# Two more plain k tiles ahead of the t2 product, and every output bank added to the residual by VectorE

## The chip, the core and the metric

The kernel runs on one core of a Trainium2 chip. The metric is device microseconds (us) from the start to the end of one execution; the time of the kernel before is the median of three runs, 2190.29 us (2189.22 to 2191.61). Five engines work side by side, each through its own queue in order: TensorE (PE, with its weight loads as PEld), VectorE (DVE), ScalarE (ACT), GpSimd (POOL) and SyncE (SP, which here only issues loads).

## The reference, cut to what matters

Two layers over a residual x of 256 rows by 2048 columns, float32. The change touches only the MLP at the end of each layer:

```python
for l in range(DEPTH):
    ...                                   # attention groups, gating, output projection, residual add
    h = rms_norm(x, mlp_norm_g[l])
    x = x + jnp.square(jax.nn.relu(h @ w_mlp_in[l])) @ w_mlp_out[l]
return rms_norm(x, final_norm_g)
```

Here h @ w_mlp_in is 256x2048 times 2048x8192, and the second product is 256x8192 times 8192x2048.

## The kernel before, in words

**Float32 by halves.** TensorE is fed float32 numbers as two rounded parts, hi and lo. For every pair of k tiles (128 rows of a weight each) of 512 columns, ScalarE copies the raw weights to hi (line 122) and VectorE writes lo = raw - hi (line 123). A product with one k tile is then three matmuls of 512 columns: activations-hi by hi, activations-lo by hi, activations-hi by lo (lines 167 to 169 in `product`, 215 to 217 in `plain`). The third of each three needs lo. The tiles hi and lo have four buffers each, so a new hi waits until TensorE has used the one four pairs earlier.

**Blocks.** The MLP runs in four chunks per layer, each of 2048 hidden columns. A chunk is four calls of `gemm7` (line 173): two that make 1024 hidden columns each, called H0 and H1 here, and two that make 1024 output columns each, called O0 and O1. A call is a block; there are 32, of some 44 us each. Names in the profile that end in h are of H blocks, names that end in o of O blocks.

**Inside a block.** Eight of the sixteen k tiles go through a scheme with seven products instead of eight on 2x2 pieces: the weight pieces b11, b12, b22, b21 (four k tiles each, 1 MB each) and sums of them, made in place by VectorE in b11 (`add`, line 200). The four output banks of PSUM are px, py, pz and pw. The other eight k tiles are plain products, in four calls of `plain(half, i)` per half of the columns, with two k tiles, one hi, one lo and twelve matmuls each. `plain(1, 0)`, `plain(1, 1)`, ... are called p10, p11, p12, p13 here. The start of a block, in the order in which it is written:

- halves of b11 and their product into px; `add(b11, b12)`; ScalarE copies px away (`keep("s1")`)
- halves of b11, now t1, and their product into py; `add(b11, b22)`; `keep("s5")`
- p10 into py and pw; halves of b11, now t2, and their product into px; `keep("v2")`
- p11, p12; the product with b22; p13; the product with t3 (b12 + b22); and so on

In H blocks b12 + b22 is made by a DMA that adds (line 229); in O blocks by VectorE (line 237), written after the product with b22, though it may run as soon as b12 and b22 are in place and b12 has been read.

**What sets the order.** Each engine takes its instructions in an order that a planner fixed when the kernel was built: by estimated times it gives each engine the earliest written instruction that is ready at that moment. So the order in the trace is not that of the text: matmuls of p10 stand among those of t1, for example. Matmuls into one bank keep their written order. `pump` lines between matmuls call pending work (the squared ReLU of the hidden columns and their turn by TensorE, lines 257 to 283).

**The output of an O block.** For each half of the columns (second half first) and each half t of the rows, the bank is scaled by r2 and added to the residual xt (lines 703 to 714): by one VectorE instruction (line 710), except for row half 1 of the first column half, which is bank px, in chunks 0 to 2: there ScalarE writes the scaled bank to a tile y (line 707) and an adding DMA that GpSimd issues adds y to xt (line 708). In the last chunk VectorE does all four. px is the last bank that a block finishes, and the following block starts at once.

Of the kernel before, what the change touches and what calls it, by code (L numbers as in the profile page):

```python
# [28 lines left out]
FCH = 4  # L29
# [12 lines left out]
def trunk(ctx: ExitStack, tc: tile.TileContext, x_in, xT, w_in, w_out, w_mlp_in, w_mlp_out,  # L42
# [22 lines left out]
    def t2(name):  # L65
        return tmp.tile([P, GW], F32, tag="t2", name=name, bufs=4)
# [95 lines left out]
    def product(ps, lhs, parts, start=False):  # L162

        for j, (hi, lo) in enumerate(parts):
            ah, al = lhs(j)
            first, last = start and j == 0, j == len(parts) - 1
            T.matmul(ps, lhsT=ah, rhs=hi, start=first, stop=False, skip_group_check=True)  # L167
            T.matmul(ps, lhsT=al, rhs=hi, start=False, stop=False, skip_group_check=True)  # L168
            T.matmul(ps, lhsT=ah, rhs=lo, start=False, stop=last, skip_group_check=True)  # L169
            if j % 2:  # L170
                pump()

    def gemm7(w, c0, lhs, sums, rest, keep, name, moved=False):

        def rawb(two, half):
            t = stage["mlp"].tile([P, SP, GW], F32, tag="rawb", name=f"rb{two}{half}_{name}", bufs=3)
            src = w[:2 * SP * P, c0 + half * GW:c0 + (half + 1) * GW].rearrange("(k two p) c -> two p k c", two=2, p=P)
            nc.sync.dma_start(t, src[two])
            return t

        def direct(k, t):
            def get(j):
                a, h = lhs[2 * j + k]
                return a[:, h, t * P:(t + 1) * P], a[:, h, S + t * P:S + (t + 1) * P]  # L190
            return get

        def summed(i):
            def get(j):
                e = sums[j]
                return e[:, 0, i], e[:, 1, i]
            return get

        def add(dst, src):
            V.tensor_tensor(dst, dst, src, op=ALU.add)  # L200

        px, py, pz, pw = (psg.tile([P, GW], F32, tag="g", name=f"p{c}_{name}") for c in "xyzw")
        raw = {}

        def plain(half, i):

            if i % 2 == 0:
                raw[half] = load(w, rest[2 * i:2 * i + 4], c0 + half * GW, f"{name}{half}{i}")
            ks = rest[2 * i:2 * i + 2]
            for k, (hi, lo) in zip(ks, halves(raw[half][:, i % 2 * 2:i % 2 * 2 + 2, :], 2, f"{name}{half}{i}")):  # L210
                a, h = lhs[k]
                for t, ps in enumerate(((pz, px), (py, pw))[half]):
                    ah, al = a[:, h, t * P:(t + 1) * P], a[:, h, S + t * P:S + (t + 1) * P]
                    first, last = k == rest[0] and t == half, k == ks[-1]
                    T.matmul(ps, lhsT=ah, rhs=hi, start=first, stop=False, skip_group_check=True)  # L215
                    T.matmul(ps, lhsT=al, rhs=hi, start=False, stop=False, skip_group_check=True)  # L216
                    T.matmul(ps, lhsT=ah, rhs=lo, start=False, stop=last, skip_group_check=True)  # L217
                pump()

        b11, b12 = rawb(0, 0), rawb(0, 1)  # L220
        product(px, direct(0, 0), halves(b11, SP, f"b11{name}"), start=True)
        add(b11, b12)
        keep("s1", px)
        b22 = rawb(1, 1)
        product(py, direct(0, 1), halves(b11, SP, f"t1{name}"), start=True)
        add(b11, b22)
        keep("s5", py)
        if moved:
            G.dma_start(b12, b22, accum_op=ALU.add)
        plain(1, 0)  # L230
        product(px, summed(0), halves(b11, SP, f"t2{name}"))
        keep("v2", px)
        plain(1, 1)
        plain(1, 2)
        product(py, summed(1), halves(b22, SP, f"b22{name}"))
        if not moved:
            add(b12, b22)
        plain(1, 3)
        product(px, summed(2), halves(b12, SP, f"t3{name}"))
        b21 = rawb(1, 0)  # L240
        keep("v3", px)
        plain(0, 0)
        add(b11, b21)
        plain(0, 1)
        product(px, direct(1, 1), halves(b11, SP, f"t4{name}"))
        plain(0, 2)
        product(pz, direct(1, 0), halves(b21, SP, f"b21{name}"))
        plain(0, 3)
        return [[pz, py], [px, pw]]
# [90 lines left out]
    for l in range(DEPTH):  # L340
# [319 lines left out]
        for c in range(FCH):  # L660
            hid, hs = [None] * KT, [None] * SP
            for g in range(2):
                kept = {}

                def keep(what, ps, kept=kept, n=f"{l}{c}{g}"):
                    k = mlp.tile([P, GW], F32, tag="kept", name=f"k{what}h{n}", bufs=4)
                    if what == "v3":
                        V.tensor_tensor(k, kept["s5"], ps, op=ALU.subtract)
                    else:
                        A.activation(k, ps, AF.Copy)  # L670
                    kept[what] = k

                ps = gemm7(w1, c * fw + 2 * g * GW, Want(xm), Want(xs), allk[2 * SP:], keep, f"h{l}{c}{g}", moved=True)
                z11, z12, z22 = kept["s1"], kept["v2"], kept["v3"]
                V.scalar_tensor_tensor(z12, z12, -1.0, ps[0][1], op0=ALU.mult, op1=ALU.add)
                V.tensor_tensor(z22, z22, ps[1][1], op=ALU.add)
                pending.append(hidden(hid, hs, ((z12, z12), (z22, z22)), 8 * g + 4, f"hid{l}{c}{g}b"))
                V.tensor_tensor(z11, z11, ps[0][0], op=ALU.add)
                pending.append(hidden(hid, hs, ((z11, z11), (ps[1][0], None)), 8 * g, f"hid{l}{c}{g}a"))
                if r2 is None:  # L680
                    rm = rstd(ss_m, f"m{l}")
                    r2 = small.tile([P, 4], F32, tag="r2", name=f"r2_{l}", bufs=2)
                    V.tensor_tensor(r2[:, :2], rm, rm, op=ALU.mult)
                    V.tensor_scalar(r2[:, 2:], r2[:, :2], -1.0, None, op0=ALU.mult)
            for g in range(2):
                def xg(t, half, g=g):
                    return xt[t][:, (2 * g + half) * GW:(2 * g + half + 1) * GW]

                kept = {}

                def keep(what, ps, kept=kept, n=f"{l}{c}{g}"):
                    k = mlp.tile([P, GW], F32, tag="kept", name=f"k{what}o{n}", bufs=4)
                    if what == "v3":
                        k = kept["s5"]
                        V.tensor_tensor(k, k, ps, op=ALU.subtract)
                        A.activation(k, k, AF.Copy, scale=r2[:, 1:2])
                    else:
                        i = {"s1": 0, "v2": 2, "s5": None}[what]
                        A.activation(k, ps, AF.Copy, **({} if i is None else {"scale": r2[:, i:i + 1]}))
                    kept[what] = k  # L700

                ps = gemm7(w2[c * fw:(c + 1) * fw], 2 * g * GW, Want(hid), Want(hs), late, keep, f"o{l}{c}{g}")
                for half in (1, 0):
                    for t in range(2):
                        if (t, half) == (1, 0) and c < FCH - 1:
                            y = t2(f"y{l}{c}{g}")
                            A.activation(y, ps[t][half], AF.Copy, scale=r2[:, t:t + 1])
                            G.dma_start(xg(t, half), y, accum_op=ALU.add)
                        else:
                            V.scalar_tensor_tensor(xg(t, half), ps[t][half], r2[:, t:t + 1], xg(t, half),  # L710
                                                   op0=ALU.mult, op1=ALU.add)
                        k = kept.get({(0, 0): "s1", (0, 1): "v2", (1, 1): "v3"}.get((t, half)))
                        if k is not None and c < FCH - 1:
                            G.dma_start(xg(t, half), k, accum_op=ALU.add)
                        elif k is not None:
                            V.tensor_tensor(xg(t, half), xg(t, half), k, op=ALU.add)
                        if c == FCH - 1:
                            square_sum(ss_a, t, 2 * g + half, f"n{l}")
                    if c == FCH - 1 and not fin:
                        q = 2 * g + half  # L720
                        pending.append(turn(xa, xt, q * GW, 4 * q, f"xa{l + 1}_{q}_", C_ATT + (l + 1) * KT))
# [75 lines left out]
```

## Time and profile before

| | before |
|---|---|
| median of three runs | 2190.29 us |
| the profiled execution, its own time | 2193.12 us |
| its span from the first to the last instruction | 2191.4 us |
| PE busy, matmuls | 2133.2 us, 97%, 9500 |
| PEld busy | 1706.9 us, 78% |
| DVE busy | 1712.0 us, 78% |
| ACT busy | 1362.8 us, 62% |
| POOL busy | 73.0 us, 3% |
| mean granted TensorE clock | 0.996 |

Busy times are shares of the span. A matmul's row lasts longer than the distance to the next one, since matmuls overlap; so a loss of TensorE is read from the starts of following matmuls. Idle time in brackets at the end of a row is the time just before it in which the engine had nothing running, with what ended it.

### The profile page before, as it was taken

What the parts mean: (1) busy time and instruction counts of PE and PEld (TensorE: products, weight loads), DVE (VectorE), ACT (ScalarE), POOL (GpSimd) and SP (SyncE); (2) the same over time, 40 slices, a digit from 0 to 9 for tenths busy, and PEclk for the clock granted to TensorE, in tenths of its full rate; (3) what the DMA queues carried; (4) which work ended last, traced back from release to release, by engine and by line L of the source; (5) the groups of instructions that cost most, each with busy time, mean ns of one, the idle gap of its engine ahead of it and who ended that gap; (6) DMA issues with size and microseconds to landing.
All of it is one profiled execution on the core that took longest, in us unless ns stands there. A gap on an engine that the chain in (4) does not pass through costs nothing. (4 is left out here: it accounts for less than half of the span.)

```text
span 2191.4 us, 25750 instructions
## 1 busy us (share of the span) xinstructions
PE 2133.2 (97%) x9500; PEld 1706.9 (78%) x9500; DVE 1712.0 (78%) x2024; ACT 1362.8 (62%) x1903; POOL 73.0 (3%) x90
## 2 busy tenths in 40 slices
PE   9999999999999999999999999999999999999996
PEld 7877888777777777777788778887777777777775
DVE  6665566898898898889965655678988988988897
ACT  6465565675675576667654656556656755755764
POOL 0000000000000000000000000000000000000000
PEclk9999999999999999999999999999999999999999
DMA  8644565567857866766465454656677578568652
GB/s 317 203 144 156 168 229 169 180 212 228 236 167 212 258 207 187 213 217 203 155 215 183 143 157 155 241 147 218 212 225 202 193 231 248 173 192 253 209 191 96
DMA packets 212621, 435.35 MB, mean 199 GB/s; under 512 B 7824, under 2 KB 8464, under 8 KB 210320
## 3 DMA queue, kind: packets, MB, share of 16 engines
q1 hardware_dynamic: 202416, 402.22, 55.9%
q0 software_dynamic: 9216, 29.36, 7.0%
q10 hardware_dynamic: 864, 2.14, 0.3%
q8 instruction: 74, 1.21, 0.2%
q14 instruction: 51, 0.42, 0.1%
HBM read 402.23 MB, written 2.10 MB: 185 GB/s over the span
## 5 line engine op out<-in xcount | busy, mean ns | idle before, releaser
L123 DVE TENSOR_TENSOR lo_wi<-raw_wi,hi_wi 128x1024 fp32r<-128x1024 f32 x160 | 195.1, 1223 | 162.2 <-ACT hi_wi L122 154.6
L122 ACT ACTIVATE hi_wi<-raw_wi 128x1024 fp32r<-128x1024 f32 x160 | 168.9, 1059 | 166.7 <-PE pg_wi L157 156.1
L156 PE MATMUL pg_wi<-hi_wi,xa 128*128 128x512 f32 x640 | 260.4, 407 | 0.0
L158 PE MATMUL pg_wi<-lo_wi,xa 128*128 128x512 f32 x640 | 251.6, 393 | 0.0
L157 PE MATMUL pg_wi<-hi_wi,xa 128*128 128x512 f32 x640 | 251.3, 393 | 0.0
L122 ACT ACTIVATE hi_o<-raw_o 128x1024 fp32r<-128x1024 f32 x128 | 134.8, 1058 | 64.9 <-PE pw_o L216 43.1
L123 DVE TENSOR_TENSOR lo_o<-raw_o,hi_o 128x1024 fp32r<-128x1024 f32 x128 | 153.9, 1222 | 17.7 <-ACT hi_o L122 16.7
L122 ACT ACTIVATE hi_h<-raw_h 128x1024 fp32r<-128x1024 f32 x128 | 134.2, 1054 | 46.9 <-PE pw_h L216 24.4
L123 DVE TENSOR_TENSOR lo_h<-raw_h,hi_h 128x1024 fp32r<-128x1024 f32 x128 | 154.8, 1220 | 7.2 <-ACT hi_h L122 7.2
L200 DVE TENSOR_TENSOR rb_o<-rb_o,rb_o 128x2048 f32<-128x2048 f32 x64 | 146.4, 2288 | 9.6 <-DMA rb_o<-w_mlp_out 9.0
L156 PEld LDWEIGHTS pg_wi<-hi_wi,xa 128*128 128x128 f32 x640 | 120.3, 188 | 29.1 <-issue 7.3
L158 PEld LDWEIGHTS pg_wi<-lo_wi,xa 128*128 128x128 f32 x640 | 120.4, 188 | 25.2
L157 PEld LDWEIGHTS pg_wi<-hi_wi,xa 128*128 128x128 f32 x640 | 120.5, 188 | 22.3 <-issue 0.7
L123 DVE TENSOR_TENSOR lo_wo<-raw_wo,hi_wo 128x1024 fp32r<-128x1024 f32 x64 | 78.4, 1225 | 60.8 <-ACT hi_wo L122 60.8
L200 DVE TENSOR_TENSOR rb_h<-rb_h,rb_h 128x2048 f32<-128x2048 f32 x48 | 109.8, 2288 | 1.3 <-DMA rb_h<-w_mlp_in 0.8
L122 ACT ACTIVATE hi_wo<-raw_wo 128x1024 fp32r<-128x1024 f32 x64 | 67.9, 1060 | 64.0 <-PE pg_wo L157 57.8
L156 PE MATMUL pg_wo<-hi_wo,mix 128*128 128x512 f32 x192 | 76.3, 397 | 0.0
L158 PE MATMUL pg_wo<-lo_wo,mix 128*128 128x512 f32 x192 | 75.1, 391 | 0.0
L157 PE MATMUL pg_wo<-hi_wo,mix 128*128 128x512 f32 x192 | 74.8, 389 | 0.0
L123 DVE TENSOR_TENSOR lo_b11h<-rb_h,hi_b11h 128x1024 fp32r<-128x1024 f32 x32 | 39.2, 1226 | 27.8 <-ACT hi_b11h L122 25.9
L123 DVE TENSOR_TENSOR lo_t1h<-rb_h,hi_t1h 128x1024 fp32r<-128x1024 f32 x32 | 38.7, 1224 | 23.8 <-ACT hi_t1h L122 23.8
L123 DVE TENSOR_TENSOR lo_t3o<-rb_o,hi_t3o 128x1024 fp32r<-128x1024 f32 x32 | 39.0, 1224 | 23.4 <-ACT hi_t3o L122 23.3
(1939 smaller groups left out, 5880.9 us busy)
## 6 DMA issues: line engine op xcount, KB each, us to landing
raw_wi<-w_in SPq DMA_DIRECT2D x80, 1024.0 KB, 5.2
rb_h<-w_mlp_in SPq DMA_DIRECT2D x64, 1024.0 KB, 6.2
raw_h<-w_mlp_in SPq DMA_DIRECT2D x64, 1024.0 KB, 5.6
raw_o<-w_mlp_out SPq DMA_DIRECT2D x64, 1024.0 KB, 6.6
rb_o<-w_mlp_out SPq DMA_DIRECT2D x64, 1024.0 KB, 6.5
raw_wo<-w_out SPq DMA_DIRECT2D x24, 1024.0 KB, 5.1
rb_h<-rb_h POOLq DMA_DIRECT2D x16, 1024.0 KB, 6.9
raw_wo<-w_out SPq DMA_DIRECT2D x16, 512.0 KB, 5.0
```

The lines of the kernel that those rows point to most:

```text
L122: A.activation(hi, raw[:, i:i + m, :], AF.Copy)
L123: V.tensor_tensor(lo, raw[:, i:i + m, :], hi.bitcast(F32), op=ALU.subtract)
L156: T.matmul(ps[t], lhsT=ah, rhs=hi, start=first, stop=False)
L157: T.matmul(ps[t], lhsT=al, rhs=hi, start=False, stop=False)
L158: T.matmul(ps[t], lhsT=ah, rhs=lo, start=False, stop=last)
L200: V.tensor_tensor(dst, dst, src, op=ALU.add)
```

## The change

`plain(1, 1)`, p11, is written ahead of the product with t2 and no longer behind it, in all 32 blocks. The banks px of the O blocks in chunks 0 to 2 (twelve of them) are added to the residual by VectorE in place of ScalarE and the adding DMA.

```diff
         plain(1, 0)
+        plain(1, 1)
         product(px, summed(0), halves(b11, SP, f"t2{name}"))
         keep("v2", px)
-        plain(1, 1)
         plain(1, 2)
...
                     for t in range(2):
-                        if (t, half) == (1, 0) and c < FCH - 1:
-                            y = t2(f"y{l}{c}{g}")
-                            A.activation(y, ps[t][half], AF.Copy, scale=r2[:, t:t + 1])
-                            G.dma_start(xg(t, half), y, accum_op=ALU.add)
-                        else:
-                            V.scalar_tensor_tensor(xg(t, half), ps[t][half], r2[:, t:t + 1], xg(t, half),
-                                                   op0=ALU.mult, op1=ALU.add)
+                        V.scalar_tensor_tensor(xg(t, half), ps[t][half], r2[:, t:t + 1], xg(t, half),
+                                               op0=ALU.mult, op1=ALU.add)
```

## Rows read from the trace of the kernel before

**Rows 1.** The page, busy us, share of the span and instructions of two engines.

```profile
PE   2133.2 (97%) x9500; PEld 1706.9 (78%) x9500; DVE 1712.0 (78%) x2024; ACT 1362.8 (62%) x1903; POOL 73.0 (3%) x90
```

**Rows 2.** Waits of PE: line and releaser, us in total, times, longest.

```profile
PE px_o L167 <- ACT hi_t2o L122: 16.8, 16, 1.6
PE px_h L169 <- DVE lo_t2h L123: 7.4, 14, 0.5
PE pw_o L215 <- ACT hi_o L122: 3.0, 7, 0.4
```

**Rows 3.** Timeline of PE in an O1: start, length, line, output and inputs.

```profile
873.01 0.50 PE L215 MATMUL pw_o<-hi_o,hid021b 128*128 128x512 f32 x1 [0.45 <-ACT hi_o L122]
...
878.55 0.39 PE L217 MATMUL pw_o<-lo_o,hid021b 128*128 128x512 f32 x1
879.44 0.50 PE L167 MATMUL px_o<-hi_t2o,e_hid020a 128*128 128x512 f32 x1 [0.50 <-ACT hi_t2o L122]
879.77 0.40 PE L168 MATMUL px_o<-hi_t2o,e_hid020a 128*128 128x512 f32 x1
880.70 0.50 PE L169 MATMUL px_o<-lo_t2o,e_hid020a 128*128 128x512 f32 x1 [0.53 <-DVE lo_t2o L123]
```

**Rows 4.** Timeline of DVE in the same O1.

```profile
869.68 0.74 DVE L710 SCALAR_TENSOR_TENSOR xt<-pz_o,r,xt 128x512 f32<-128x512 f32 x1
870.35 2.28 DVE L200 TENSOR_TENSOR rb_o<-rb_o,rb_o 128x2048 f32<-128x2048 f32 x1
872.54 2.35 DVE L123 TENSOR_TENSOR lo_t1o<-rb_o,hi_t1o 128x1024 fp32r<-128x1024 f32 x2
...
875.95 2.28 DVE L200 TENSOR_TENSOR rb_o<-rb_o,rb_o 128x2048 f32<-128x2048 f32 x1
879.42 2.36 DVE L123 TENSOR_TENSOR lo_t2o<-rb_o,hi_t2o 128x1024 fp32r<-128x1024 f32 x2 [1.18 <-ACT hi_t2o L122]
```

**Rows 5.** Timeline of ACT in the same O1.

```profile
869.43 0.69 ACT L707 ACTIVATE y<-px_o,r 128x512 f32<-128x512 f32 x1 [3.25 <-PE px_o L217]
870.01 2.00 ACT L122 ACTIVATE hi_t1o<-rb_o 128x1024 fp32r<-128x1024 f32 x2
...
876.42 0.60 ACT L699 ACTIVATE ks5o<-py_o 128x512 f32<-128x512 f32 x1 [2.89 <-PE py_o L169]
878.33 2.01 ACT L122 ACTIVATE hi_t2o<-rb_o 128x1024 fp32r<-128x1024 f32 x2 [1.31 <-DVE rb_o L200]
```

**Rows 6.** Lines 707 and 710: duration in ns (least, median, most), first and last start.

```profile
L707 ACT ACTIVATE y<-px_o,r x12: 690/691/691, 511.7 to 1998.9; 128x512 f32<-128x512 f32 x12
L710 DVE SCALAR_TENSOR_TENSOR xt<-px_o,r,xt x4: 740/746/751, 1048.1 to 2177.1; 128x512 f32<-128x512 f32 x4
```

**Rows 7.** Timeline of PE at t2 in an H0, an H1 and an O0.

```profile
742.62 0.50 PE L167 MATMUL px_h<-hi_t2h,e_xm 128*128 128x512 f32 x1 [0.26 <-ACT hi_t2h L122]
743.88 0.50 PE L169 MATMUL px_h<-lo_t2h,e_xm 128*128 128x512 f32 x1 [0.52 <-DVE lo_t2h L123]
...
789.16 0.50 PE L169 MATMUL px_h<-lo_t2h,e_xm 128*128 128x512 f32 x1 [0.53 <-DVE lo_t2h L123]
...
832.81 0.56 PE L167 MATMUL px_o<-hi_t2o,e_hid020a 128*128 128x512 f32 x1 [1.63 <-ACT hi_t2o L122]
```

**Rows 8.** Timeline of DVE in that H0 and that O0.

```profile
735.72 2.36 DVE L123 TENSOR_TENSOR lo_t1h<-rb_h,hi_t1h 128x1024 fp32r<-128x1024 f32 x2 [0.67 <-ACT hi_t1h L122]
742.60 2.36 DVE L123 TENSOR_TENSOR lo_t2h<-rb_h,hi_t2h 128x1024 fp32r<-128x1024 f32 x2 [1.19 <-ACT hi_t2h L122]
...
828.97 2.28 DVE L200 TENSOR_TENSOR rb_o<-rb_o,rb_o 128x2048 f32<-128x2048 f32 x1
831.17 1.22 DVE L123 TENSOR_TENSOR lo_o<-raw_o,hi_o 128x1024 fp32r<-128x1024 f32 x1
```

**Rows 9.** Busy us in windows, PE PEld DVE ACT POOL, clock, DMA: O0's start, and behind its wait.

```profile
814.00:837.00 23.00, 21.11 (x92) 16.84 (x91) 22.83 (x21) 17.04 (x24) 0.00 (x0) 0.93 0.41 134
...
833.00:836.50 3.50, 3.50 (x9) 2.78 (x9) 3.50 (x4) 1.75 (x3) 0.00 (x0) 0.52 0.02 5
```

## The prediction

> **What bounds the kernel now.** I read the page first, then the waits of TensorE, then the timelines around those waits. The page has TensorE busy for 97% of the span [rows 1], and the kernel has almost nothing else to wait for, so only the places where TensorE stands still can be won back. The waits of PE put nearly all of them at one spot: the first matmuls of the product with t2, which wait for ScalarE's hi (16.8 us) or VectorE's lo (7.4 us in H blocks) [rows 2]. The reader is to see in both rows the same few waits repeated, 16 and 14 times.
>
> The timelines show why. t2 is made in place: VectorE adds b22 to b11 in 2.28 us, which it can only do after lo of t1; then ScalarE makes hi, then VectorE lo. In the O1 shown the add starts at 875.95, hi at 878.33 and lo at 879.42, and VectorE sits idle for 1.18 us before that lo [rows 4, 5]. TensorE has run out of t1 and p10 by 878.55 [rows 3].
>
> A wait costs more than its printed idle time. Following matmuls start 0.23 us apart. From 878.55 to 879.44 are 0.89 us, so 0.66 are lost where 0.50 are printed; from 879.77 to 880.70 are 0.93, so 0.70 for 0.53 [rows 3]. I add 0.17 to every printed idle time below.
>
> **The swap, by kind of block.** p11 adds and removes no instruction. It puts 12 matmuls, 12 x 0.23 = 2.76 us, between p10 and t2, and one hi and one lo ahead of t2's. Two things must hold for it to pay: p11's own halves must be there in time, and what they push back must not be late in turn.
> - Halves: p11's raw weights come with the load of p10. Its hi can go into idle time of ScalarE (2.89 us before 876.42 [rows 5]). Its lo, half of the 2.36 us that two take, comes behind the add, because the add is written earlier; there it falls into the 1.18 us (O1) or 1.19 us (H0) in which VectorE waits for hi of t2 anyway [rows 4, 8]. So lo of t2 is hardly later than now, and the cover is as long as the lo that it hides: were that idle time gone, lo of t2 would be 1.2 us later, which the 2.76 us of p11 still cover.
> - p11's lo is ready some 1.2 us after the add's end, when TensorE has just finished p10. Four of p11's matmuls (two per bank) need hi alone, 0.92 us, so I leave 0.1 to 0.15 us of each wait standing.
>
> H0: waits of 0.26 and 0.52 [rows 7], with two times 0.17 they make 1.12; gain 1.0 each. The 14 waits on lo in H blocks [rows 2] are those of all eight H1 and of six H0 (the H0 of each layer's first chunk shows none): 6.0 us. H1: 0.53 + 0.17 = 0.70, and some tenths among the turns beside it [rows 7]; gain 0.75, eight blocks: 6.0 us. O1 of chunks 0 to 2: 0.66 + 0.70 = 1.36 [rows 3]; gain 1.2, six blocks: 7.2 us. The two O1 of the last chunks have other work between and wait less regularly; bounds 0 and 1.36, I take 0.4: 0.8 us.
>
> O0 is different, and I expect little there. Its wait is the largest, 1.63 + 0.17 = 1.8 us, in eight blocks [rows 7]. But VectorE is busy for 22.83 of the 23 us around it [rows 9], and there the add (828.97) comes ahead of lo of p10 (831.17) [rows 8]. Matmuls of p11 go into the same two banks as p10's and stand behind those that need this lo, which ends only at 832.4, 0.4 us before the wait ends now. So p11 can't fill that wait; bounds are 0 and 1.8, nearest to the rows is 0.4 at most, and I take 0.2: 8 x 0.2 = 1.6 us.
>
> What is late next? The product with b22 and those behind it have their hi bound by free buffers, which TensorE frees, and p12 stays where it was, so nothing behind t2 gets less cover but `keep("v2")`: px is next written by the t3 product, with p12, b22 and p13 between, 36 matmuls or 8.3 us, for a copy like the 0.60 us of `keep("s5")` at 876.42 [rows 5]. I count nothing.
>
> **The second edit.** It removes 12 ScalarE writes of 0.69 us and 12 adding DMAs that nobody waits for, and adds 12 VectorE instructions of 0.75 us [rows 6]. Before the next of its kind starts, one takes 0.67 us (869.68 to 870.35 [rows 4]). Where do they fall? At the start of the next block, behind the one for pz.
> - In the six H0 that follow, VectorE then idles for 0.67 us (735.72 [rows 8]), since ScalarE's y delays hi of t1. The new instruction fills just that: nothing either way.
> - In the six O1, ScalarE's y (869.43) delays hi of t1 and of p10 [rows 5], for which TensorE waits 0.45 + 0.17 = 0.62 us at 873.01 [rows 3]; in total the waits' row has 3.0 us [rows 2]. That wait may go. Against it, VectorE has no idle time there: the add of b12 and b22 (870.35) and lo of t1 (872.54) [rows 4] come 0.67 us later if they keep their order; if the planner finds hi of t1 ready and puts the add behind it, lo of t1 comes 872.54 - 870.35 - 0.67 = 1.5 us earlier. So a block lies between 0.67 lost and 0.62 gained. The wait is a row and the delay only a possibility, so I stay near the row, at 0.5: 3.0 us.
>
> The Trainium skill speaks against this edit: "VectorE: DVE Perf Modes", Specifications, has "VectorE sits closer to SBUF; ScalarE sits closer to PSUM", so that ScalarE would be the engine to empty a bank. The trace agrees, with 0.75 against 0.69 us [rows 6]; by that alone the edit would lose 12 x 0.06 = 0.7 us, if it lay on the path.
>
> **Sum.** 6.0 + 6.0 + 7.2 + 0.8 + 1.6 + 3.0 = 24.6 us. From the profiled execution's 2193.1 us this leaves 2168.5. The median of the runs is 2190.3, 2.8 lower, so I forecast 2165.7.
>
> **The rivals.**
> 1. The O0 wait goes too. If the planner puts lo of p10 ahead of the add there, as the other blocks have it (for O1 the gap from 874.9 to 875.95 [rows 4] is that lo), TensorE has p10 and p11 to do while t2 is made: 8 x 1.6 more instead of 0.2, 11.2 us, and the clock drop that can follow this wait (3.5 us at a granted clock of 0.52, the lower of the two levels, where it is else 1.00 [rows 9]; 1.7 us each time) goes as well. Time 2165.7 - 11.2 = 2154.5 or somewhat less. For it: order is the planner's to choose, and it has p11 to weigh now. Against: neither edit touches what stands ahead of that add in an O0, which follows an H1.
> 2. The wait only changes its name, from t2's halves to p11's lo. If p11's matmuls of hi are not spread over both banks, or its hi is planned late, TensorE waits some 0.7 us at line 217 in the 20 blocks counted for the swap: 14 us less gain, 2179.7. For it: p11's lo stands behind the same add. Against: ScalarE's idle time and the four matmuls without lo.
> 3. Slower: VectorE bounds the start of the blocks. If every microsecond of VectorE there goes through to TensorE, the swap gains nothing, as it changes VectorE's order and not its work, and the second edit costs 12 x 0.67 = 8.0 us: 2198.3. It decides from the point where VectorE has no idle time between lo of t1 and lo of t2. For it: 22.83 of 23 us in O0 [rows 9]. Against: the idle 1.18 and 1.19 us [rows 4, 8], in the blocks where I count most of the gain.
> 4. The change doesn't do what it says: the planner's estimates let t2's matmuls stand ahead of p11's anyway, as it does in O0 with p10's (832.81 is followed by matmuls of p10). Then the time stays, 2190.3.
>
> **How the numbers follow.** Forecast 0.52, rival 1 0.15, rival 2 0.17, rival 3 0.10, rival 4 0.06. The forecast's own range goes up by the second edit at its bound in O1 (6 x 1.17 = 7.0 us) and by nothing gained in O0 and the last two O1 (2.4), to 2175; and down by O0 at 0.4 (1.6), the last two O1 at 1.36 (1.9), the second edit at 0.62 (0.7) and nothing left of the waits at p11 (20 x 0.12 = 2.4), to 2159. To hold 8 in 10 I leave out rivals 3 and 4 and a little at the lower end: 2151 to 2187. A change under 0.2%, 4.4 us, can't be told from none in this kernel's measurement. Faster: 0.52 + 0.15 + 0.17 = 0.84; same 0.06; slower 0.10.
>
> **What would show it.** The waits of PE for hi and lo of t2 in H0, H1 and O1 gone from the list of waits, with at most 0.2 us each on p11's lo; VectorE's idle time before lo of t2 filled by a lo of p11; the O0 wait still there at line 167 or 217, eight times, of 1.2 to 1.8 us. For the second edit: bank px added by VectorE right behind pz, and in O1 the lo of t1 directly behind both, ahead of the add of b12 and b22. The prediction is wrong if new waits of PE at p11 add up to more than 5 us, if the O0 waits vanish, or if the b12 + b22 add turns up between lo of p11 and lo of t2, so that t2 waits again.

## The result, and the profile after

| | before | after |
|---|---|---|
| median of four runs | 2189.76 us (2188.17 to 2191.61) | 2157.11 us (2156.86 to 2160.34) |
| the profiled execution | 2193.12 us | 2156.94 us |

The ratio is 0.9854, with a 95% interval of 0.9837 to 0.9871: 32.7 us faster, where 24.6 were forecast.

The page of the kernel after, busy us, share and instructions; the answer to [rows 1]:

```profile
PE 2115.4 (98%) x9500; PEld 1707.6 (79%) x9500; DVE 1717.3 (80%) x2036; ACT 1354.7 (63%) x1891; POOL 65.3 (3%) x78
```

TensorE does the same 9500 matmuls. VectorE has 12 instructions more and ScalarE and GpSimd 12 fewer each.

The waits of PE in the kernel after (line and releaser, us in total, times, longest); the answer to [rows 2]:

```profile
PE px_o L167 <- ACT hi_t2o L122: 10.1, 9, 1.3
PE px_o L215 <- DVE ks5o L695: 5.9, 15, 0.6
PE py_o L215 <- ACT ks5o L699: 3.0, 9, 1.2
PE pz_o L217 <- DVE lo_o L123: 0.8, 1, 0.8
PE pw_o L215 <- ACT hi_o L122: 0.3, 1, 0.3
```

The wait on lo of t2 in H blocks (7.4 us) is gone. That on hi of t2 is left nine times, and eight of these are the O0 blocks. Of the seven waits for hi of p10 one is left. The second row is the price: before, this wait came 7 times for 2.6 us in all, now 15 times. It is the first plain product into px behind t3, which must wait until VectorE has subtracted the t3 product into `kept` (line 695); I call it the v3 wait.

**Where the time went, by block.** I take each block from its first matmul with b11 to that of the next block, in the two profiled executions. The H0 blocks are shorter by 9.5 us in all (1.3 to 1.4 each in the regular ones), the eight H1 by 8.2 (1.02 each), the six O1 of chunks 0 to 2 by 16.9 (2.8 each), and the very last O1 with its tail by 2.6. The O0 are longer: by 0.5 to 0.7 in six of them, which makes 3.4. The other two are shorter by 1.1 each, because before they held a drop of the granted clock ([rows 9] is one, at 0.52; the other, from 1918.0 to 1921.5, stands at 0.58). In all O0 lose 1.2 us. These, with 0.2 ahead of the first block, make 36.2 us, the difference of the two spans. The execution profiled before was 3.4 us above its median; its two drops make 3.0 of them (those O0 took 47.1 us, the other six 45.6).

Now the same places as in the rows of before. VectorE at the start of an O1 of the kernel after (start, length, line, operation, output and inputs), the answer to [rows 4]:

```profile
856.87 0.74 DVE L705 SCALAR_TENSOR_TENSOR xt<-pz_o,r,xt 128x512 f32<-128x512 f32 x1
857.53 0.74 DVE L705 SCALAR_TENSOR_TENSOR xt<-px_o,r,xt 128x512 f32<-128x512 f32 x1
858.19 2.35 DVE L123 TENSOR_TENSOR lo_t1o<-rb_o,hi_t1o 128x1024 fp32r<-128x1024 f32 x2
860.46 1.22 DVE L123 TENSOR_TENSOR lo_o<-raw_o,hi_o 128x1024 fp32r<-128x1024 f32 x1
861.59 2.28 DVE L200 TENSOR_TENSOR rb_o<-rb_o,rb_o 128x2048 f32<-128x2048 f32 x1
863.79 1.22 DVE L123 TENSOR_TENSOR lo_o<-raw_o,hi_o 128x1024 fp32r<-128x1024 f32 x1
864.93 2.28 DVE L200 TENSOR_TENSOR rb_o<-rb_o,rb_o 128x2048 f32<-128x2048 f32 x1
867.13 2.35 DVE L123 TENSOR_TENSOR lo_t2o<-rb_o,hi_t2o 128x1024 fp32r<-128x1024 f32 x2
```

The reader is to see three things. px is added right behind pz. lo of t1 comes directly behind both, where before the 2.28 us add of b12 and b22 stood between (870.35 in [rows 4]). And that add now stands at 864.93, between lo of p11 and lo of t2. Idle time there is none.

TensorE in the same O1, the answer to [rows 3]:

```profile
867.25 0.40 PE L217 MATMUL pw_o<-lo_o,hid021b 128*128 128x512 f32 x1
867.49 0.39 PE L167 MATMUL px_o<-hi_t2o,e_hid020a 128*128 128x512 f32 x1
867.72 0.39 PE L168 MATMUL px_o<-hi_t2o,e_hid020a 128*128 128x512 f32 x1
867.95 0.40 PE L215 MATMUL py_o<-hi_o,hid021a 128*128 128x512 f32 x1
...
868.65 0.40 PE L169 MATMUL px_o<-lo_t2o,e_hid020a 128*128 128x512 f32 x1
```

The last matmul of p11 and the first of t2 are 0.24 us apart: no wait, where 0.66 and 0.70 us were lost before. The first lo of t2, at 868.65, stands behind three matmuls of p12 (867.95 is the first).

TensorE's waits in the O0 ahead of it, the answer to the last of [rows 7]:

```profile
818.93 0.50 PE L215 MATMUL py_o<-hi_o,hid021b 128*128 128x512 f32 x1 [0.23 <-ACT ks5o L699]
820.91 0.50 PE L167 MATMUL px_o<-hi_t2o,e_hid020a 128*128 128x512 f32 x1 [1.24 <-ACT hi_t2o L122]
841.77 0.50 PE L215 MATMUL px_o<-hi_o,hid021b 128*128 128x512 f32 x1 [0.34 <-DVE ks5o L695]
```

The 1.63 us wait has become 1.24, and two short ones have come beside it. Read by starts against the regular 0.23 us, and with the 0.1 us by which the matmul behind a wait is late too, the loss at t2 fell from 1.8 to 1.5, that at py rose from 0.16 to 0.50, and the v3 wait adds 0.61 that was not there.

### The profile page after: what moved, and what is told of

It is laid out like the page before. It is cut to its first block, busy times and chain, and to the rows that moved or that the text cites. A ratio compares the mean times of both kernels' runs of the same rounds, so it can differ in the third digit from the quotient of the medians.

```text
span 2155.2 us, 25746 instructions
## 1 busy us (share of the span) xinstructions
PE 2115.4 (98%) x9500; PEld 1707.6 (79%) x9500; DVE 1717.3 (80%) x2036; ACT 1354.7 (63%) x1891; POOL 65.3 (3%) x78
## 5 line engine op out<-in xcount | busy, mean ns | idle before, releaser
L122 ACT ACTIVATE hi_b11h<-rb_h 128x1024 fp32r<-128x1024 f32 x32 | 34.0, 1063 | 33.9 <-PE px_h L216 13.3
```

The source lines that it names most:

```text
L122: A.activation(hi, raw[:, i:i + m, :], AF.Copy)
```

## The experiments

Each is a change to the kernel after, unless it says that it undoes a part. The differences of time are those of medians. The kernel before, measured again beside them, took 2191.04 us beside the swap alone, the second edit alone, the edit of p10 and the DMA in all O blocks; 2191.97 beside the kernel without px additions, the swap with a DMA, the copy by ScalarE and the three together; and 2191.32 beside the two fillers. That is up to 2.2 us from the 2189.76 above, so a difference of 1 to 2.4 us from the kernel after rests on the lengths of the blocks in the traces, and the medians only agree with them.

### The swap alone

The output of px goes back to ScalarE and the adding DMA; p11 stays ahead of t2.

> p11 ahead of t2; bank px in chunks 0 to 2 still goes through ScalarE and the adding DMA. Theory A (the two edits add up, each with what the changed kernel shows of it): the swap alone gives H0 6 x 1.3, H1 8 x 1.0, O1 6 x 1.3 and O0 about nothing, 23 us less than before, 2166; in O1 the wait of 0.45 us at 873 stays, and the 0.50 and 0.53 us at t2 go. Theory B (the swap does nearly all, the second edit's VectorE instruction is only hidden): 30 us or more less than before, 2160 or below.

2168.23 us (2167.5 to 2169.12), ratio 0.99 (0.9885 to 0.9915): 22.8 us less than before. H0 gives 8.9, H1 8.1, the six O1 6.8 (1.1 each) and the very last one 2.4; O0 loses 0.7 in sum, which is 0.5 in each of the six undisturbed ones, less what the two drops of before gave back. In O1 the t2 waits are gone and those at t1 stay. VectorE and the wait at the same place:

```profile
685.61 0.74 DVE L710 SCALAR_TENSOR_TENSOR xt<-pz_o,r,xt 128x512 f32<-128x512 f32 x1
686.27 2.28 DVE L200 TENSOR_TENSOR rb_o<-rb_o,rb_o 128x2048 f32<-128x2048 f32 x1
688.47 2.35 DVE L123 TENSOR_TENSOR lo_t1o<-rb_o,hi_t1o 128x1024 fp32r<-128x1024 f32 x2
```

```profile
688.93 0.50 PE L215 MATMUL pw_o<-hi_o,hid011b 128*128 128x512 f32 x1 [0.45 <-ACT hi_o L122]
```

This is the order and the wait of before, to a hundredth [rows 3, 4]. The time is near the 23 us of Theory A. It is also near the 21.6 us that the prediction's terms for the swap make, but that is partly luck: H0, H1 and the last O1 gave 6.7 us more than forecast, and the eight O0, at 0.5 lost each, 5.5 less. The rest of the 32.7 us isn't the swap's.

### The second edit alone

p11 goes back behind t2; VectorE adds px.

> Bank px added by VectorE in all chunks; p11 stays behind t2. Theory A (additive): 9 us less than before, 2181, all of it in the six O1 blocks (1.5 us each). Theory C (the edits need each other: on VectorE the add of b12 and b22 is now planned between the add of b11 and b22 and lo of t2, 2.28 us where 1.18 were idle, and only p11 covers that): the O1 blocks win some 0.9 us at t1 and lose 1.1 us at t2, so 2188 to 2191, with a wait of PE for lo of t2 in O1 of 1.2 to 1.8 us. Forecast of the prediction for this edit: 3 us less.

2187.05 us (2184.93 to 2188.86), ratio 0.9981 (0.9972 to 0.999): 4.0 us less than before. That is close to the 3.0 forecast by luck, since larger gains and losses cancel in it, and between the two theories, nearer to C. But 22.8 and 4.0 make 26.8: the two together bring 5.9 us more than one by one. The blocks say the same: the six O1 give 16.9 us with both edits, 6.8 and 3.8 with one of them. VectorE in an O1 of this kernel (x2 is two of the adds in a row), and TensorE's waits in it:

```profile
694.01 4.48 DVE L200 TENSOR_TENSOR rb_o<-rb_o,rb_o 128x2048 f32<-128x2048 f32 x2
698.41 2.35 DVE L123 TENSOR_TENSOR lo_t2o<-rb_o,hi_t2o 128x1024 fp32r<-128x1024 f32 x2
```

```profile
697.50 0.50 PE L167 MATMUL px_o<-hi_t2o,e_hid010a 128*128 128x512 f32 x1 [0.23 <-ACT hi_t2o L122]
699.39 0.50 PE L215 MATMUL py_o<-hi_o,hid011b 128*128 128x512 f32 x1 [1.16 <-ACT hi_o L122]
```

Here too the add of b12 and b22 has left its place ahead of lo of t1, and the t1 waits (1.3 us per O1) are gone. But it now stands right ahead of lo of t2, and TensorE loses 1.9 us around t2 where it lost 1.6 before, and 0.3 more than before at v3. The long wait printed is on hi of p11 and not on lo of t2, as Theory C had it; but lo of t2 was there only 0.2 us later (698.41 and half of 2.35 us, an estimate). With p11 ahead of t2 the 12 matmuls cover this; that is the interaction.

### Is it VectorE's work or its order: px not added at all

```diff
-                        V.scalar_tensor_tensor(xg(t, half), ps[t][half], r2[:, t:t + 1], xg(t, half),
-                                               op0=ALU.mult, op1=ALU.add)
+                        if (t, half) != (1, 0) or c == FCH - 1:
+                            V.scalar_tensor_tensor(...)
```

> The changed kernel with the twelve additions of bank px in chunks 0 to 2 left out, so that part of the output is missing; neither ScalarE nor VectorE has that work. Theory work (the new VectorE instruction costs up to the 0.67 us that it takes): 0 to 8 us less than the changed kernel, 2149 to 2157. Theory order (the instruction's place is worth more than its time: with it, hi of t1 is ready when VectorE comes free and lo of t1 goes ahead of the 2.28 us add of b12 and b22; without it the planner puts that add first again): slower than the changed kernel, by some 1 us in each of six O1 blocks, 2161 to 2164.

2168.34 us (2166.76 to 2168.97), ratio 0.9894 (0.9879 to 0.9909). With less work it is 11.2 us slower than after. Theory order had the direction right and the size too small (2161 to 2164): an O1 takes 1.7 us more than after, not some 1. VectorE and ScalarE in an O1:

```profile
686.19 0.75 DVE L706 SCALAR_TENSOR_TENSOR xt<-pz_o,r,xt 128x512 f32<-128x512 f32 x1
686.85 2.28 DVE L200 TENSOR_TENSOR rb_o<-rb_o,rb_o 128x2048 f32<-128x2048 f32 x1
689.05 2.35 DVE L123 TENSOR_TENSOR lo_t1o<-rb_o,hi_t1o 128x1024 fp32r<-128x1024 f32 x2
```

```profile
686.39 2.01 ACT L122 ACTIVATE hi_t1o<-rb_o 128x1024 fp32r<-128x1024 f32 x2 [3.70 <-DVE rb_o L200]
```

The add is back ahead of lo of t1, although ScalarE has no y to make. ScalarE starts hi of t1 at 686.39; one of its two instructions takes 1.05 us, so the first half stands at about 687.4 (an estimate from rows). VectorE comes free of pz at 686.85, before that, and the planner gives it the add. With 0.67 us of px behind pz it comes free after it, and lo of t1 is what it gets. These are times of the trace; the planner's own estimates are not on record.

### A filler in the place of the px addition

The 12 instructions stay, with the same shape and length, but read bank pz and write a tile that nobody reads.

```diff
-                        V.scalar_tensor_tensor(xg(t, half), ps[t][half], r2[:, t:t + 1], xg(t, half),
+                        d, u = xg(t, half), t
+                        if (t, half) == (1, 0) and c < FCH - 1:
+                            d, u = t2(f"y{l}{c}{g}"), 0
+                        V.scalar_tensor_tensor(d, ps[u][half], r2[:, u:u + 1], xg(t, half),
```

> The changed kernel without the addition of bank px in chunks 0 to 2 (so part of the output is missing), and in its stead a VectorE instruction of the same form that reads bank pz again and writes a tile that nobody reads. On VectorE it stands where the addition stood, behind that of pz and ahead of lo of t1; the add of b12 and b22 comes later, as in the changed kernel. Theory order (all that the second edit wins is that hi of t1 gets ready in its time): as fast as the changed kernel, 2155 to 2159, although nothing is done. Theory bank (it is bank px being emptied by VectorE that helps): as slow as with the addition left out, 2166 to 2170.

2158.58 us (2157.64 to 2163.32), ratio 0.9857 (0.984 to 0.9875): as fast as after, 9.8 us faster than without any instruction there. Its O1:

```profile
684.52 0.74 DVE L708 SCALAR_TENSOR_TENSOR xt<-pz_o,r,xt 128x512 f32<-128x512 f32 x1
685.19 0.74 DVE L708 SCALAR_TENSOR_TENSOR y<-pz_o,r,xt 128x512 f32<-128x512 f32 x1
685.85 2.35 DVE L123 TENSOR_TENSOR lo_t1o<-rb_o,hi_t1o 128x1024 fp32r<-128x1024 f32 x2
```

A useless instruction brings what the px addition brings. ScalarE's writes of y and the adding DMAs are gone from this kernel and from the one without px additions alike. So what is worth some 10 us is neither the bank, nor ScalarE's relief, nor the DMAs, but 0.67 us of VectorE at this spot, which changes what follows.

### The same filler, reading the slice of xt that pz was just added to

The edit is that of the filler above, with `xg(u, half)` at the end of the line.

> The same as the filler in place, but it also reads what the addition of pz has just written, so the planner puts it between the two lo of t1, with the add of b12 and b22 ahead of both. Theory order: not faster than with the addition left out, 2168, and slower by up to 6 x 0.67 = 4 us: 2166 to 2173. Theory work (what counts is VectorE's work and not its order): the same as the filler in place.

2186.82 us (2185.27 to 2189.19), ratio 0.998 (0.997 to 0.9989). The expectation was missed by far, and for a reason of its own. VectorE in an H0:

```profile
743.57 0.75 DVE L708 SCALAR_TENSOR_TENSOR y<-pz_o,r,xt 128x512 f32<-128x512 f32 x1 [1.59 <-DMA xt<-ks1o]
744.24 1.22 DVE L123 TENSOR_TENSOR lo_h<-raw_h,hi_h 128x1024 fp32r<-128x1024 f32 x1
745.37 2.35 DVE L123 TENSOR_TENSOR lo_t2h<-rb_h,hi_t2h 128x1024 fp32r<-128x1024 f32 x2
```

The slice that the filler reads also gets an adding DMA (`ks1o`). The filler waited for that, and the queue of VectorE behind it: lo of p11 came late, and TensorE waited for it in six H0, 11.0 us in all. So the total decides nothing. In O1 the filler fell between the two lo of t1, behind the add of b12 and b22, and waited for the DMA some 0.2 us in most of them; there only 0.2 us per block was gained over before, where the swap alone gives 1.1. In these blocks the same work costs 0.9 us at one place (0.2 of it the wait for the DMA) and gains at the other, as the order theory has it.

### The swap, with O1's b12 + b22 by a DMA

The px output stays with ScalarE, as in the swap alone; the O1 calls get `moved=g == 1`, so that the disputed add leaves VectorE.

> The swap alone, with bank px still through ScalarE and y, and b12 + b22 made by an adding DMA in O1 only, so that on VectorE lo of t1 follows the add of bank pz directly. Theory order: the O1 blocks win what the second edit won there beside the swap, 1.4 to 1.7 us each, 8 to 10 us less than the swap alone, 2158 to 2160, although ScalarE still makes y first. Theory ScalarE (y, which delays hi of t1 and of p10, is what holds O1's start): the wait of PE for hi of p10 at line 215 stays, and 4 us at most are won, 2164 or more.

2161.47 us (2161.04 to 2163.04), ratio 0.9863 (0.9847 to 0.988): 6.8 us less than the swap alone, and 1.5 more than Theory order allowed. O1 gains 2.2 each in place of 1.1. VectorE in it:

```profile
684.67 0.74 DVE L710 SCALAR_TENSOR_TENSOR xt<-pz_o,r,xt 128x512 f32<-128x512 f32 x1
686.08 2.36 DVE L123 TENSOR_TENSOR lo_t1o<-rb_o,hi_t1o 128x1024 fp32r<-128x1024 f32 x2 [0.67 <-ACT hi_t1o L122]
```

ScalarE's y still delays hi of t1, and VectorE idles for 0.67 us; yet the t1 waits of TensorE are gone. So what made them in O1 was the add ahead of lo of t1, and not the y that the prediction blamed. By starts, the v3 wait of O1 stays at 0.9 us or more here, as in the swap alone; in the kernel after it is 0.45. That part of the second edit's gain does not come with the add's move alone, and what makes it is not shown.

### O0: lo of p10 ahead of the add

`add(b11, b22)` is written behind p10 and no longer ahead of `keep("s5")`.

> The changed kernel, with p10 written ahead of the add of b22 to b11, so that VectorE makes lo of p10 before that add in O0 too. Theory order (the wait left in O0 is there because lo of p10 stands behind the add): TensorE runs p10 while the add and hi of t2 are made, p11 covers the rest, and 1.2 to 1.6 of the 1.8 us lost per O0 go: 10 to 13 us less than the changed kernel, 2144 to 2147. Theory capacity (VectorE has no free time in O0, so what is put ahead makes something else late): the wait moves to lo of p11 or to hi of t2, under 3 us, 2154 to 2158. H blocks: the same order as now on VectorE, no change.

2155.52 us (2155.28 to 2156.82), ratio 0.9842 (0.9825 to 0.9858), 1.6 less than after. In O0 lo of p10 does come ahead of the add, and the loss at t2 falls from 1.5 to 1.1 us, no further. Each O0 is 0.35 us shorter than after, each O1 0.1 longer. The order of these two is not what holds O0.

### O0: the b12 + b22 add by a DMA

All O calls get `moved=True`.

> The changed kernel, with b12 + b22 made by an adding DMA in O blocks too, which takes 2.28 us off VectorE in each of 16 blocks. Theory capacity: the O0 wait goes, 8 x 1.8 = 14 us less than the changed kernel, 2143, and O1, which waits for nothing there, stays. Theory order: on VectorE lo of p10 still stands behind the add in O0, but with hi of t1 as the limit the add runs earlier; of the 1.8 us 0.5 to 1.0 go, 4 to 8 us, 2149 to 2153. If the DMA (1 MB, some 7 us) lands later than hi of t3 needs it, t3 waits: up to 16 x 2 us more, 2157 to 2189.

2156.04 us (2155.25 to 2156.76), ratio 0.9844 (0.983 to 0.9859), 1.1 less than after. None of the three forecasts was met. Each O0 gains 0.6, each O1 loses some 0.5, in the v3 wait (8.9 us in all blocks). The first waits of PE in this kernel:

```profile
PE px_o L215 <- DVE ks5o L695: 8.9, 15, 0.9
PE py_o L217 <- DVE lo_o L123: 5.1, 8, 0.6
```

2.28 us less of VectorE's work ahead of t2 end the wait on hi of t2 in O0, and lo of p10 takes its place, eight times 0.6. Neither work nor order of VectorE alone accounts for O0.

### The v3 wait: ScalarE empties px

```diff
-                        k = kept["s5"]
-                        V.tensor_tensor(k, k, ps, op=ALU.subtract)
+                        k, v = kept["s5"], t2(f"v3{n}")
+                        A.activation(v, ps, AF.Copy)
+                        V.tensor_tensor(k, k, v, op=ALU.subtract)
```

> The changed kernel, with bank px emptied by ScalarE after t3 in O blocks (a copy to a tile, from which VectorE subtracts later), since PE now waits 15 times for VectorE's subtraction from that bank, 5.9 us printed and some 0.17 more each. If VectorE's queue is what makes the bank late: 5 to 8 us less than the changed kernel, 2149 to 2152. If ScalarE's queue (two hi of t4) makes it as late: the wait changes its releaser, under 2 us.

2154.72 us (2154.22 to 2155.12), ratio 0.9833 (0.9818 to 0.9848): 2.4 less than after, half of the least that was expected. O0 lost its v3 wait (0.55 each, 4.5 in all), but in O1 the copy comes later than VectorE's subtraction did, and 0.35 each (2.1) went back.

### The three together

The add of O0 alone by DMA (`moved=g == 0`), lo of p10 ahead of the add, and px emptied by ScalarE.

> The changed kernel with three edits more: b12 + b22 by DMA in O0 only, p10 written ahead of the add of b22 to b11, and bank px emptied by ScalarE after t3 in O blocks. If they add up as they were seen alone (0.6 us per O0 for the first, some 0.4 for the second, 5 to 8 us for the third): 10 to 15 us less than the changed kernel, 2142 to 2147. If the second and the first win the same wait: 2147 to 2150.

2150.82 us (2150.41 to 2151.3), ratio 0.9815 (0.9801 to 0.983), 6.3 less than after: the fastest of all, and a little above both ranges. Each O0 takes 45.0 us, 0.6 less than before and 1.1 less than after. That is what the DMA (0.6) and the copy by ScalarE (0.55) gave alone; the edit of p10 adds nothing here, since the add comes ahead of lo of p10 all the same. VectorE in an O0, and the waits:

```profile
639.11 1.22 DVE L123 TENSOR_TENSOR lo_t1o<-rb_o,hi_t1o 128x1024 fp32r<-128x1024 f32 x1 [0.93 <-ACT hi_t1o L122]
...
641.84 2.29 DVE L200 TENSOR_TENSOR rb_o<-rb_o,rb_o 128x2048 f32<-128x2048 f32 x1
...
645.35 1.22 DVE L123 TENSOR_TENSOR lo_o<-raw_o,hi_o 128x1024 fp32r<-128x1024 f32 x1
```

```profile
PE py_o L217 <- DVE lo_o L123: 5.1, 8, 0.6
PE px_o L215 <- ACT v L695: 4.0, 7, 0.7
```

## Why the prediction was right, and where it was not

**The range.** 2157.1 us lies within the 2151 to 2187 that were stated, but below the forecast's own 2159 to 2175. The stated range reached that far down for the sake of rival 1, which did not come; what brought the time there is the second edit, whose term was outside its own bounds. So the time came inside partly by luck.

**The swap in H0 and H1: right, a little small.** 1.3 and 1.02 us each for 1.0 and 0.75. A wait costs more than the 0.17 that I added: the matmul behind the one that waited starts 0.33 us after it and not 0.23 (879.44 to 879.77 in [rows 3]), so the loss beyond the printed idle time is 0.27. H0's two waits then make 1.32.

**The swap in O1: the mechanism right.** 1.1 each for 1.2. The t2 waits of 1.57 us went, and 0.4 came back on average as a longer v3 wait (0.2 to 0.6 over the six blocks).

**What is late next: this step failed.** I looked behind t2 at `keep("v2")` alone and counted nothing. TensorE reaches the end of t3 earlier now, and VectorE does not: the subtraction of line 695 is late. By starts, this costs 0.7 us in an O0 and 0.35 in an H1 (line 668 there), where nothing stood before: 8.5 us over the sixteen blocks of the kernel after. In an O1 of the swap alone it costs 0.4 more than before. In the O0 of the kernel after, VectorE's timeline shows why:

```profile
835.41 2.29 DVE L200 TENSOR_TENSOR rb_o<-rb_o,rb_o 128x2048 f32<-128x2048 f32 x1 [0.60 <-DMA rb_o<-w_mlp_out]
837.62 2.36 DVE L123 TENSOR_TENSOR lo_o<-raw_o,hi_o 128x1024 fp32r<-128x1024 f32 x2
839.90 1.22 DVE L123 TENSOR_TENSOR lo_t4o<-rb_o,hi_t4o 128x1024 fp32r<-128x1024 f32 x1
841.03 0.68 DVE L695 TENSOR_TENSOR ks5o<-ks5o,px_o 128x512 f32<-128x512 f32 x1
```

The add waits 0.60 us for a load of weights. That load is issued right behind the last lo of b22, at 829.29, which is 18.9 us into the block, and takes 6.1 us. In an O0 of before it is issued 18.3 us into the block, at 662.03, takes 6.1 us as well, and the same two instructions start without a wait:

```profile
668.23 2.29 DVE L200 TENSOR_TENSOR rb_o<-rb_o,rb_o 128x2048 f32<-128x2048 f32 x1
...
673.84 0.68 DVE L695 TENSOR_TENSOR ks5o<-ks5o,px_o 128x512 f32<-128x512 f32 x1
```

So the subtraction starts 30.6 us into the block where it started at 30.1, and TensorE starts the plain product into px only when it is done, at 841.77. What makes the subtraction late in an H1 is not shown.

**O0: the wait stayed, as forecast.** Eight times at t2, 1.5 by starts, within the 1.2 to 1.8 named. The gain there is 0.3 for the 0.2 taken, but the block is longer for the waits at py and v3, so that +1.6 us became -3.4 over the six undisturbed ones (-0.57 each). Rival 1 is out: the waits are there. The drop of the clock that it coupled to them is not in the profiled execution after; it is in one O0 each of the second edit alone, the kernel without px additions and the swap with a DMA, and in no O0 of the others; in the filler that waited for a DMA it is in two H0. A wait of that length can be followed by one and mostly isn't.

**The last two O1: 0.8 forecast, 2.6 measured.** The very last one had waits of 1.16 us on the hi of a plain product and of 1.03 on lo of t3, which I did not price; one of 0.82 is left in their place.

**The second edit: the mis-sized term.** 3.0 us forecast, 11.1 measured (swap alone against after, by medians; 10.1 by the six O1 of the traces). That is 1.7 us per O1, where the bounds were 0.67 lost and 0.62 gained. Two things were wrong in it. First, the price: I took the one wait of 0.62 us at 873.01, but by starts the t1 waits of that O1 make 1.32, since smaller ones on lo of t1 and behind it follow that the waits' row for hi doesn't hold; and the v3 wait is 0.45 us shorter than in the swap alone, which no term had. Second, the branch: I left open whether the planner would put lo of t1 ahead of the add, and it could be read. Without y, hi of t1 starts as soon as the add ahead of it ends; after the add of 2.28 us, VectorE spends 0.67 on pz and 0.67 on px, 1.34 us, and half of hi of t1 takes 1.05. So lo of t1 is ready when VectorE comes free, and without px it is not. Experiments without px, with the filler, and with the add taken out of VectorE's queue show the three sides of this.

**The sign that I named against myself came up.** The add does stand between lo of p11 and lo of t2, and t2 does not wait: p11, and three matmuls of p12, cover it. In the second edit alone, where they don't, TensorE loses 1.9 us around t2.

**Rivals 2 to 4.** No new wait at p11's lo in H0, H1 or O1: rival 2 is out. Rival 3, VectorE's work passed on to TensorE, would have made the kernel without px additions faster than after; it is 11.2 us slower. Rival 4 is out by the time.

**Open.** What holds O0 at its last 1 us is not settled. When VectorE has less to do, the wait goes from hi of t2 to lo of p10. In the fastest kernel VectorE then stands idle for 0.93 us for ScalarE's hi of t1 (639.11), and ScalarE, which has the squared ReLU of the block before ahead of it, runs from 637.50 to 648.06 without a break. That points at ScalarE; no run tried it.

## What to carry to other kernels

Where a planner fixes the order, an instruction's length also decides what its engine takes next: price an edit by what comes free at which moment, against when each candidate is ready, and not by its duration alone. Test a gain that is larger than its mechanism with a filler of the same length, and both edits alone: here the filler was worth 9.8 us, and the two edits, each alone, gave 5.9 us less than together. And when work is moved ahead of a wait, follow TensorE to every later bank that another engine must empty first: cover taken from there comes back as a wait.

## What was not expected of the hardware

- A matmul that waited costs twice: its own start, and 0.10 us more to the next one (0.33 in place of 0.23), so that a printed wait of 0.50 is a loss of 0.77.
- The granted clock fell to the lower of its two levels, 1.2 and 2.4 GHz (0.52 and 0.58 as means of 3.5 us), behind a 1.6 us wait of TensorE in two of eight O0 of one execution. It did so in one O0 of three other kernels (waits of 1.2 to 1.6 us), in two H0 of the filler that waited for a DMA (waits of up to 2.4 us), and behind none of the other waits at these spots (0.6 to 1.7 us).
- An instruction of VectorE that reads a slice to which a DMA adds is made to wait for that DMA: 1.59 us in the filler's H0, and all that was queued behind it on VectorE waited too.
